# The end of a 128-tile Strassen matmul: where the last weight sets are put, how the last block of C21 is added, and how it is stored

## The chip, the cores and the metric

One NeuronCore of a Trainium2 chip runs the whole program. TensorE (PE) multiplies, VectorE (DVE) and ScalarE (ACT) scale, add and copy, SyncE (SP) issues the DMAs. The metric is the device time of one execution in microseconds (us). The kernel before takes 1450.54 us, the median of 3 runs from 1450.36 to 1450.79.

## The reference

`x` is 8 x 2048 x 2048 and `w` is 2048 x 2048, both float32. The cumulative sum of `x` along the sequence, less the same sum moved on by one place, is `x` again, so what is computed is a matrix product:

```python
cs = np.cumsum(x, axis=1)
diff = cs - np.concatenate([np.zeros((cs.shape[0], 1, cs.shape[2]), dtype=np.float32), cs[:, :-1, :]], axis=1)
return np.matmul(diff, w).astype(np.float32)
```

The kernel takes `x` as 16384 rows, that is 128 tiles of 128 rows, and multiplies them by `w`.

## The kernel before, in words

Four row tiles are done plainly in bf16. Then come 31 groups of four tiles (`g`, `g+1`, `h = g+2`, `h+1`), in float16 with a scale for each row. A group is one Strassen-Winograd step over 2 x 2 blocks: `A11`, `A12` are the two halves (in K) of tiles `g` and `h`, `A21`, `A22` those of `g+1` and `h+1`, and `B11` to `B22` the quarters of `w`. Products named P1 to P5 go one level further: `Quarters` makes each from seven quarter products (`slot(0)` to `slot(6)`), each of four 128 x 512 matmuls, and two products (T2 and T3) are plain, in pieces of four matmuls. So PE does 51 pieces of four matmuls in each group.

Weights of the inner level are differences of blocks of `w`. Most lie ready. One set at a time (`Q1`, `Q3` or `Q4`) is made on DVE just before it is needed (`give`, one 128 x 2048 subtraction) and written to `flow`, a buffer of four pieces that all these sets share. A set can be written when the matmuls that read the set before it are done.

Inside `Quarters`, `h[0]` is a bank that collects the quarter products 0, 2, 4 and 6. After product 0 ACT copies it to `g[0]` (`first`). After products 2 and 4 ACT copies what it holds so far to a lent buffer (`out2`, `out4`), and DVE adds those copies to `g[1]` and `h[1]` (`middle`, `last`). Product 6 changes `h[0]` for the last time, so it must come after `out4`.

The results of a group leave PSUM by scaled copies on ACT (`keep`, line 624), followed by scaled adds on DVE (`add`, line 635), and are stored by SP (`put`). The last group stores 128 x 512 pieces of 256 KB (line 655), the others 512 KB. In every group C21 of tile `h+1` is the last: ACT keeps `Y` in SBUF, and after product 6 of P4 DVE adds `P4.h` times the row scale. In the kernel before its half 0 is the last instruction of DVE, and its store the last of the program.

The order of the work is not that of the code. Every step is recorded with a label and an engine, and `emit` sorts all of them by a table of numbers (`places`), one list for each group: 0, 1, 2, 29, 30, 31 and one for all between. Group 30 is the last, and list 31 holds what is left of its end. In that order each engine runs its own steps strictly in turn; the framework adds the waits. Where DVE and ACT both touch one PSUM bank, it lets the later of the two wait for the earlier, for reads too.

These are the last steps of each engine in the kernel before, in their order (a bare name is of group 30):

```
PE   ... P4.2, S3h T3.1.0, P4.1, S3h T3.1.1, S3h T3.0.0, S3h T3.0.1, P4.4, P4.3, P4.5, P4.6
DVE  ... in4.Q3, P4.s3, P4.middle, P4.s4, C22h+Y.1, C22h+Y.0, P4.last, C21h+P4.h.1, C21g+P4.g.1, C21g+P4.g.0, C21h+P4.h.0
ACT  ... P4.out2, keep C21h.1, keep C21h.0, P4.out4, keep C21g.1
SP   ... put3.1.1 (C22h), put3.1.0, put-1.0.1 (C21h), put1.0.1 (C21g), put1.0.0, put-1.0.0 (C21h)
```

`S3h T3.1.x` fill bank `Y[1]` and `S3h T3.0.x` bank `Y[0]`; `P4.0`, `P4.2`, `P4.4`, `P4.6` fill `P4.h[0]`.

For the start of the last group these names matter too. `load7.0` brings half of the last row tile, `weigh7.0` sums it on ACT, `narrow7.0` makes it float16 and `turn7.0` transposes it by DMA. They belong to the tiles of group 30 but run at the end of group 29, between steps of both groups.

Of the kernel before, what the change touches and what calls it, by code (L numbers as in the profile page):

```python
# [10 lines left out]
def kernel(  # L11
# [103 lines left out]

    def record(label, engine, ask):
        at = seen[period[0], label] = seen.get((period[0], label), 0) + 1
        if at > 1:
            label = f"{label}#{at}"
        ops.append((period[0], label, engine, ask))  # L120

# [51 lines left out]
    def narrow_one(t, i):  # L173
        to, data, s = narrowed(t)[:, ds(i * NH, NH)], where[t][i], scales[t]
        record(
            f"narrow{role(t)}.{i}",
            "act",
            lambda: nc.scalar.activation(to, data, COPY, scale=s),  # L178
        )
        if i == 1 and t != PLAIN + 1:  # L180
            stage.append(where[t][1])
# [75 lines left out]
    def cast_x(q, a):  # L257
        to = resting(q, 0).bitcast(bf16).rearrange("p (a c) -> p a c", a=2)[:, a]
        src = resting(KH - 1 - q, a)
        record(f"cast x.{q}.{a}", "dve", lambda: nc.vector.tensor_copy(to, src))  # L260
        return to
# [13 lines left out]
    def turned(q, a, v, engine):  # L275
        to = xP[:, ds(2 * a, 2), ds(q * KQ, KQ), :].rearrange("p r k m -> p r (k m)")
        v = v.rearrange("p (r c) -> p r c", r=2)
        on = nc.scalar.copy if engine == "act" else nc.vector.tensor_copy
        record(f"turned x.{q}.{a}", engine, lambda: on(to, v))  # L279
# [30 lines left out]
    def taken(h, ko):  # L310
        src = rest(h, ko)
        to = wb[h, ko] = next(rings)
        record(f"cast w.{h}.{ko}", "act", lambda: nc.scalar.copy(to, src))
        largest(h, ko)
# [22 lines left out]
    def result(name, p, rows, columns, u=None):  # L337
        c = next(results_at)
        if u is None and name in ("out.0.1.0", "out.0.2.0"):
            record(f"{name}", "dve", lambda: nc.vector.tensor_copy(c, p))  # L340
        elif u is None:
            record(f"{name}", "act", lambda: nc.scalar.copy(c, p))  # L342
        else:
            record(f"{name}", "act", lambda: nc.scalar.activation(c, p, COPY, scale=u))
# [52 lines left out]
    for ko in range(KO - KQ):  # L397
# [20 lines left out]
        if ko == PART[-1]:  # L418
            for k in PART:
                part(k)  # L420
            record("part", "act", lambda: nc.scalar.copy(partial, banks[7]))
# [35 lines left out]
    def block(name, dst, a, h, k, engine):  # L457
        to, src = dst[k], whole[k][:, a, h, :].rearrange("p (n c) -> p n c", c=NB)
        if engine == "dve":
            ask = lambda: nc.vector.tensor_scalar(to, src, uinv, None, MUL)  # L460
        else:
            ask = lambda: nc.scalar.activation(to, src, COPY, scale=uinv)  # L462
        record(f"{name}.{k}", engine, ask)
# [159 lines left out]
    def keep_one(label, c, p, u):  # L623
        record(label, "act", lambda: nc.scalar.activation(c, p, COPY, scale=u))  # L624

    def copy(label, to, p):
        record(label, "act", lambda: nc.scalar.copy(to, p))  # L627
# [35 lines left out]
    class Seven:  # L663
# [16 lines left out]
        def give(self, name):  # L680

            p, q, op = {"Q1": ("t22", "Q2", SUB), "Q4": ("t21", "Q2", SUB), "Q3": ("Q2", "t11", SUB)}[name]
            if name == "Q4":
                less(f"{self.name}.{name}", passed, self.b[p], self.b[q])
            else:
                tensor(f"{self.name}.{name}", flow, self.wide[p], self.wide[q], op)
            self.b[name] = passed

        def spill(self, name):
# [3 lines left out]
            what = flow if self.b[name] is passed else self.wide[name]  # L693
# [122 lines left out]

    def group_plain(g):
# [69 lines left out]
        make_2(in_2)  # L887
# [16 lines left out]
        make_3(in_3)  # L904
# [18 lines left out]
    def all_seven(g):  # L923
        return g > PLAIN + 4

# [3 lines left out]
    def first_two(g):  # L929
        if g < END:  # L930
# [3 lines left out]
            if all_seven(g):  # L934
# [3 lines left out]
            ready[2] = Quarters("P2", ready["zz"], A12g, A12h, in_2, room(at + 1), False)  # L938

    def group(g):  # L940
        h = g + 2
        more = all_seven(g)
# [30 lines left out]
        if more:  # L973
# [29 lines left out]
        P5 = Quarters("P5", P2.banks, S1g, S1h, in_5, room(at))  # L1003
# [12 lines left out]
        if not more:  # L1016
            make_5(in_5)
        in_5.give("Q3")
# [15 lines left out]
        if not more:  # L1034
            make_1(in_1)
# [7 lines left out]
        P3 = Quarters("P3", P5.banks, S4g, S4h, in_3, room(at + 1))  # L1043
# [12 lines left out]
        in_3.give("Q1")  # L1056
# [20 lines left out]
        P4 = Quarters("P4", P3.banks, A22g, A22h, in_4, room(at))  # L1077
        P4.one()
        P4.two()
        in_3.give("Q3")  # L1080
        if not more:
            make_3(in_4)
# [19 lines left out]
        in_4.give("Q1")  # L1102
# [19 lines left out]
        in_4.give("Q3")  # L1122
# [25 lines left out]
        if next_g < END:  # L1148
            if all_seven(g + 4):
# [8 lines left out]
        C21h = keep("keep C21h", Y, vh, halves=[0])  # L1158
        add("C22h+Y", C22h, Y, vh, [0])
        keep("keep C21h", Y, vh, C21h, [1])  # L1160
        add("C22h+Y", C22h, Y, vh, [1])
        P4.slot(6)
        turn(next_l, [1])
# [3 lines left out]
        def tail():  # L1167
            add("C21h+P4.h", C21h, P4.h, vh, [0])
# [8 lines left out]
    for g in range(PLAIN + 4, END, 4):  # L1177
# [405 lines left out]
```

## Time and profile before

| what | value |
|---|---|
| median of 3 runs | 1450.54 us |
| span of the profiled execution, first to last instruction | 1449.2 us |
| PE busy | 1438.6 us, 99% |
| DVE busy | 1334.3 us, 92% |
| ACT busy | 1204.5 us, 83% |
| DMA, mean | 243 GB/s |
| last PE piece | from 1443.10 us |
| last store issued | at 1445.68 us |

The page gives the span of the execution that was profiled; of that execution no other time is given. The runs timed without a profile lie 1.3 us above the span. The page cuts the span into 40 slices, gives the share of each engine in each, and follows the chain of work that ended last. A timeline gives start and duration of each instruction, and in square brackets how long its engine had been idle before it and who ended that. One row may stand for several instructions of one line (`x4`): then its duration is that of the whole row, in which pipelined instructions overlap.

### The profile page before, as it was taken

To read this page: it belongs to the slowest core of one execution; us is meant where nothing else is said; L and a number is where in the kernel's file an instruction comes from. 1 tells how busy PE (TensorE), PEld (TensorE's weight loads), DVE (VectorE), ACT (ScalarE), POOL (GpSimd) and SP (SyncE) were. 2 spreads that over 40 slices of the span, in tenths; PEclk is the share of its full clock that TensorE was granted. 3 is DMA by queue.
4 is the path that set the end of the run, shared out by engine and by line. 5 is a ranking of instruction groups with operands and counts; after the bars stand their busy time and mean duration, and the time that the engine had idled before them with its cause. 6 is when DMAs were issued, how large, how long until landed. Compare 5 with 4: busy or idle time off the path is not lost.

```text
span 1449.2 us, 20358 instructions
## 1 busy us (share of the span) xinstructions
PE 1438.6 (99%) x6692; PEld 652.2 (45%) x6698; DVE 1334.3 (92%) x2345; ACT 1204.5 (83%) x1994; POOL 0.5 (0%) x5
## 2 busy tenths in 40 slices
PE   8999999999999999999999999999999999999998
PEld 4444444444444444444444444444444444444443
DVE  6999999999999999999999999999999999999988
ACT  5997888898888888888988888988888888889783
POOL 0000000000000000000000000000000000000000
PEclk9999999999999999999999999999999999999999
DMA  9999979899888999989998888998989998989973
GB/s 360 369 252 272 252 212 228 240 247 262 226 234 226 243 262 231 244 222 228 247 265 233 228 229 237 252 257 226 222 239 244 260 248 225 218 236 248 264 200 116
DMA packets 343930, 351.59 MB, mean 243 GB/s; under 512 B 270992, under 2 KB 270992, under 8 KB 343824
## 3 DMA queue, kind: packets, MB, share of 16 engines
q1 hardware_dynamic: 343824, 350.29, 89.4%
q8 instruction: 52, 0.85, 0.2%
q14 instruction: 54, 0.44, 0.1%
HBM read 150.99 MB, written 134.22 MB: 197 GB/s over the span
## 4 chain that ended last, share of the span: by engine, by line
PE 91%; issue 4%; DMA 2%; ACT 2%; DVE 1%; DVEq 0%; POOLq 0%; ACTq 0%; SPq 0%
PE b L610 61%; PE b L588 30%; DMA x<-F 1%; DMA F<-in_x_dram 1%; DVE W L460 1%; ACT waste L140 0%; DMA out_dram<-arena 0%; ACT W L462 0%; DVE arena L635 0%; ACT arena L624 0%; ACT F L178 0%; ACT arena L342 0%; ACT arena L178 0%; DVE arena L576 0%; DVE W L576 0%
## 5 line engine op out<-in xcount | busy, mean ns | idle before, releaser
L588 PE MATMUL b<-W,x 128*128 128x512 f16 x2144 | 518.1, 379 | 0.1
L635 DVE SCALAR_TENSOR_TENSOR arena<-b,tiny,arena 128x512 f32<-128x512 f32 x612 | 446.9, 745 | 16.0 <-PE b L610 4.8
L610 PEld LDWEIGHTS <-arena 128*128 128x128 f16 x2744 | 268.2, 98 | 325.4 <-DVE arena L576 6.3
L610 PE MATMUL b<-W,arena 128*128 128x512 f16 x1672 | 413.7, 379 | 0.8 <-DVE arena L576 0.4
L624 ACT ACTIVATE arena<-b,tiny 128x512 f32<-128x512 f32 x496 | 317.0, 684 | 35.4 <-PE b L588 14.9
L588 PEld LDWEIGHTS <-x 128*128 128x128 f16 x2144 | 209.7, 98 | 253.3 <-issue 0.3
L140 ACT ACTIVATE waste<-F,tiny 128x1024 uint8<-128x1024 f32 x246 | 283.9, 1154 | 15.6 <-DMA F<-in_x_dram 14.1
L178 ACT ACTIVATE F<-F,tiny 128x1024 f16<-128x1024 f32 x246 | 282.1, 1147 | 10.9 <-DVE tiny L163 9.4
L610 PE MATMUL b<-W,x 128*128 128x512 f16 x1192 | 287.5, 379 | 0.0
L610 PE MATMUL b<-arena 128*128 128x512 f16 x1072 | 261.6, 379 | 0.0
L610 PEld LDWEIGHTS <-x 128*128 128x128 f16 x1428 | 139.7, 98 | 168.5
L576 DVE TENSOR_TENSOR b<-b,arena 128x512 f32<-128x512 f32 x298 | 205.9, 691 | 5.7 <-ACT arena L627 2.0
L627 ACT COPY b<-b 128x512 f32<-128x512 f32 x149 | 85.5, 574 | 134.4 <-PE b L610 112.4
L627 ACT COPY arena<-b 128x512 f32<-128x512 f32 x298 | 170.2, 580 | 19.9 <-PE b L610 13.0
L576 DVE TENSOR_TENSOR arena<-W 128x2048 f16<-128x2048 f16 (+1 forms) x158 | 185.6, 1176 | 0.4 <-PE b L610 0.4
L576 DVE TENSOR_TENSOR arena<-x,x 128x512 f16<-128x512 f16 (+1 forms) x181 | 91.5, 506 | 50.1 <-PE b L610 50.1
L576 DVE TENSOR_TENSOR x<-x,x 128x1024 f16<-128x1024 f16 x124 | 85.2, 687 | 2.0
L576 DVE TENSOR_TENSOR arena<-W,arena 128x512 f16<-128x512 f16 (+1 forms) x157 | 85.9, 563 | 0.6 <-PE b L610 0.5
L576 DVE TENSOR_TENSOR arena<-arena 128x512 f16<-128x512 f16 x120 | 50.8, 424 | 13.7 <-PE b L610 11.8
L610 PE MATMUL b<-arena,x 128*128 128x512 f16 x236 | 60.3, 379 | 0.0
L324 PE MATMUL b<-arena 128*128 128x512 bf16 x234 | 53.5, 379 | 1.5 <-DVE arena L279 0.8
L576 DVE TENSOR_TENSOR arena<-x,arena 128x512 f16<-128x512 f16 x119 | 49.6, 417 | 0.6 <-PE b L610 0.6
(49 smaller groups left out, 503.6 us busy)
## 6 DMA issues: line engine op xcount, KB each, us to landing
F<-in_x_dram SPq DMA_DIRECT2D x246, 512.0 KB, 5.4
out_dram<-arena SPq DMA_DIRECT2D x240, 512.0 KB, 4.8
W<-in_w_dram SPq DMA_DIRECT2D x31, 512.0 KB, 9.5
out_dram<-arena SPq DMA_DIRECT2D x31, 256.0 KB, 2.7
W<-in_x_dram SPq DMA_DIRECT2D x16, 256.0 KB, 6.6
x<-F SPq DMA_TRANSPOSE x246, 4.4
arena<-in_x_dram SPq DMA_DIRECT2D x2, 512.0 KB, 5.1
W<-in_w_dram SPq DMA_DIRECT2D x2, 256.0 KB, 9.0
```

Source lines behind the costliest of these rows:

```text
L140: lambda: nc.scalar.activation(waste, data, ABS, bias=least, scale=1.0 / ROW, accum_out=m),
L178: lambda: nc.scalar.activation(to, data, COPY, scale=s),
L324: said = nc.tensor.matmul(to[n], xP[:, r, ko, :], b[:, ds(n * NB, NB)], start=(ko == 0), stop=(ko == KO - 1),)
L460: ask = lambda: nc.vector.tensor_scalar(to, src, uinv, None, MUL)
L576: record(label, "dve", lambda: nc.vector.tensor_tensor(dst, p, q, op))
L588: said = nc.tensor.matmul(to[n], a[k], b[k][:, n, :], start=(start and k == 0), stop=(k == KH - 1), skip_group_check=True,)
L610: said = nc.tensor.matmul(to, a[k], b[k], start=(start and k == 0), stop=(k == 3), skip_group_check=True)
L624: record(label, "act", lambda: nc.scalar.activation(c, p, COPY, scale=u))
L627: record(label, "act", lambda: nc.scalar.copy(to, p))
L635: label, "dve", lambda: nc.vector.scalar_tensor_tensor(c, p, u, c, MUL, ADD)
```

## The change

- In the last group the sets `in3.Q1`, `in3.Q3`, `in4.Q1` and `in4.Q3` are no longer written to `flow`, but each to a block of weights of its own that P1 and P2 have used and that no later group needs (`home`). In all other groups nothing changes here.
- Half 0 of `C21h` in the last group: ACT copies `Y[0]` unscaled to SBUF (`copy C21h`), DVE adds this to `P4.h[0]` in its bank (`C21h+P4.h0`) after `out4` and before product 6. After product 6 ACT scales and copies the left 256 columns of the bank (`end.0`), DVE the right 256 (`end.1`). Two stores of 128 x 256, 128 KB each, follow, one issued by ACT (`put end.0`), one by SP (`put end.1`). The scaled add of half 0 (`C21h+P4.h.0`) and its store of 256 KB are gone.
- The lists 29, 30 and 31 are new: in the last two groups the steps stand in another order on PE, DVE, ACT and SP. On PE the pieces are the same. Up to the first pieces of group 29 all four orders are as before.
- Helpers are rewritten so that a step can be recorded for either engine (`on_two`, `moved`), and products can be made plain (`plainly`, `made`); the tables in this kernel leave all engines and products as they were.

```diff
+        final = g + 4 >= END
+        over = [in_1.wide["t11"], in_1.wide["t21"], in_2.wide["t11"], in_2.wide["t21"]]
+        def home():
+            return over.pop(0) if final else flow
...
-        in_3.give("Q3")
+        if not P3.plain:
+            in_3.give("Q3", home())
...
+        if final:
+            C21h = free.pop(0)
+            copy("copy C21h", C21h[:, 0, :], Y[0])
+            add("C22h+Y", C22h, Y, vh, [0])
+            keep("keep C21h", Y, vh, C21h, [1])
+            add("C22h+Y", C22h, Y, vh, [1])
+            tensor("C21h+P4.h0", P4.h[0], P4.h[0], C21h[:, 0, :], ADD)
...
         def tail():
+            if final:
+                P4.last()
+                add("C21h+P4.h", C21h, P4.h, vh, [1])
+                put_half(C21h[:, 1, :], h + 1, 0, 1)
+                for i, engine in enumerate(("act", "dve")):
+                    columns = ds(i * NB // 2, NB // 2)
+                    c, p = C21h[:, 0, columns], P4.h[0][:, columns]
+                    record(f"end.{i}", engine, on_two(c, p, vh))
...
```

The last steps of each engine in the changed kernel, in their order:

```
PE   ... P4.0, S3g T3.0.0, P4.2, P4.1, S3g T3.0.1, P4.4, S3h T3.1.0, S3h T3.1.1, S3h T3.0.0, S3h T3.0.1, P4.5, P4.3, P4.6
DVE  ... P4.s3, P4.middle, C22g+X.0, P4.s4, P4.last, C22h+Y.1, C21h+P4.h.1, C22h+Y.0, C21h+P4.h0, C21g+P4.g.1, C21g+P4.g.0, end.1
ACT  ... P4.out2, P4.out4, keep C21g.0, keep C21h.1, copy C21h, keep C21g.1, end.0, put end.0
SP   ... put3.1.1, put-1.0.1, put3.1.0, put1.0.1, put1.0.0, put end.1
```

The waits that the framework adds: `copy C21h` waits for `C22h+Y.0` (same bank), `keep C21h.1` for `C22h+Y.1`, `P4.6` for `C21h+P4.h0`, and `end.1` for `end.0`.

Around the seam of groups 29 and 30 these orders are new (before, then after):

```
SP   before: load5.1, turn6.0, turn4.1, put0.1, turn6.1, put2.1, load7.0, load7.1, put1.1, turn5.1, put1.0, turn5.0
SP   after:  load5.1, turn4.1, put0.1, turn6.0, turn6.1, put2.1, load7.0, load7.1, turn5.0, turn5.1, put1.1
ACT  before: keep C21h.0, P4.out4, unit6, keep C21h.1, 30:P1.first, weigh7.0, weigh7.1
ACT  after:  P4.out4, weigh7.0, keep C21h.1, keep C21h.0, 30:P1.first, weigh7.1, 30:P1.out2
DVE  after:  C22h+Y.0, C21g+P4.g.0, P1.s2, 30:in1.Q4.0, C22h+Y.1, P2.s2, C21g+P4.g.1, 30:P4.last, ... 30:C11g+P2.g.0
PE   after:  29:P4.4, S3h T3.1.1, P4.3, P4.6, P4.5, then 30:P1.1, P1.0, P2.0, P1.2, P2.1, P1.3, ... P2.4, S2g T2.0.0, P5.0
```

`P5.0` of group 30 writes the bank that `C11g+P2.g.0` reads.

More of the change, by code (lines that the diff above doesn't have):

```diff
@@ L114 @@
     seen = {}
+    moved = {
+    }
     def record(label, engine, ask):
@@ L119, in record, with on_two @@
             label = f"{label}#{at}"
+        if isinstance(ask, dict):
+            if label in moved.get(period[0], ()):
+                engine = {"act": "dve", "dve": "act"}[engine]
+            ask = ask[engine]
         ops.append((period[0], label, engine, ask))
+    def on_two(to, src, scale=None):
+        if scale is None:
+            return {
+                "act": lambda: nc.scalar.copy(to, src),
+                "dve": lambda: nc.vector.tensor_copy(to, src),
+            }
+        return {
+            "act": lambda: nc.scalar.activation(to, src, COPY, scale=scale),
+            "dve": lambda: nc.vector.tensor_scalar(to, src, scale, None, MUL),
+        }
     def role(t):
@@ L335, with result @@
     results_at = iter(results * 2)
-    def result(name, p, rows, columns, u=None):
+    def result(name, p, rows, columns):
         c = next(results_at)
[L339 to L344, printed above, removed]
+        record(name, "dve" if name in ("out.0.1.0", "out.0.2.0") else "act", on_two(c, p))
         done.append(
@@ L420 @@
                 part(k)
[L421 removed]
+            record("part", "act", on_two(partial, banks[7]))
     for ko in range(KO - KQ, KO):
@@ L678, in room, with give @@
             return [spare.pop(0) for _ in range(4)]
-        def give(self, name):
+        def give(self, name, to=flow):
             p, q, op = {"Q1": ("t22", "Q2", SUB), "Q4": ("t21", "Q2", SUB), "Q3": ("Q2", "t11", SUB)}[name]
+            pieces = [to[:, k, :] for k in range(4)]
             if name == "Q4":
-                less(f"{self.name}.{name}", passed, self.b[p], self.b[q])
+                less(f"{self.name}.{name}", pieces, self.b[p], self.b[q])
             else:
-                tensor(f"{self.name}.{name}", flow, self.wide[p], self.wide[q], op)
-            self.b[name] = passed
+                tensor(f"{self.name}.{name}", to, self.wide[p], self.wide[q], op)
+            self.b[name] = pieces
         def spill(self, name):
@@ L692, in spill @@
             spilled.append(to)
-            what = flow if self.b[name] is passed else self.wide[name]
+            what = flow
             record(f"{self.name}.{name}.spill", "sp", lambda: nc.sync.dma_start(to, what))
@@ L815, in slot, with plainly, made @@
                 matmuls(*halves_of(f"{self.name}{name}", to, a, self.right, True)[at % 4])
+    def plainly(name, g):
+        return name in {PLAIN + 4: ('P1',)}.get(g, ())
+    making = {}
+    def made(name, inner, how):
+        if name not in making:
+            making[name] = True
+            how(inner)
     def group_plain(g):
@@ L972, in group @@
         P1.slot(1)
-        if more:
+        if not P1.plain:
             in_1.give("Q4")
@@ L1015, in group @@
         P1.slot(6)
-        if not more:
-            make_5(in_5)
-        in_5.give("Q3")
+        if not P5.plain:
+            made("P5", in_5, make_5)
+            in_5.give("Q3")
         C11h = keep("keep C11h", Y, uh, free.pop(1))
@@ L1033, in group @@
         total("S4g", S4g, A12g, S2g, SUB)
-        if not more:
-            make_1(in_1)
+        if not plainly("P1", g + 4):
+            made("P1", in_1, make_1)
+        if not plainly("P2", g + 4):
+            made("P2", in_2, make_2)
         go(2)
@@ L1101, in group @@
         P3.last()
-        in_4.give("Q1")
+        if not P4.plain:
+            in_4.give("Q1", home())
         scale_of(next_k)
@@ L1121, in group @@
             ready[1].two()
-        in_4.give("Q3")
+        if not P4.plain:
+            in_4.give("Q3", home())
         weigh(next_l, [0])
@@ L1157, in group @@
         turn(next_l, [0])
[L1158 to L1161, printed above, removed]
-        P4.slot(6)
+        if final:
[5 more added lines that the diff above has]
+            tensor("C21h+P4.h0", P4.h[0], P4.h[0], C21h[:, 0, :], ADD)
+        else:
+            C21h = keep("keep C21h", Y, vh, halves=[0])
+            add("C22h+Y", C22h, Y, vh, [0])
+            keep("keep C21h", Y, vh, C21h, [1])
+            add("C22h+Y", C22h, Y, vh, [1])
+        P4.slot(6)
+        if P4.plain and not plainly("P4", g + 4):
+            made("P4", in_4, make_3)
+        if P5.plain and not plainly("P5", g + 4):
+            made("P5", in_5, make_5)
+        if P3.plain and not plainly("P3", g + 4):
+            made("P3", in_3, make_3)
         turn(next_l, [1])
@@ L1167, in tail @@
         def tail():
+            if final:
[6 more added lines that the diff above has]
+                    record(f"end.{i}", engine, on_two(c, p, vh))
+                for i in range(2):
+                    columns = ds(i * NB // 2, NB // 2)
+                    c = C21h[:, 0, columns]
+                    record(
+                        f"put end.{i}",
+                        ("act", "sp")[i],
+                        lambda queue=(nc.scalar, nc.sync)[i], c=c, columns=columns: queue.dma_start(
+                            out2[ds((h + 1) * P, P), columns], c
+                        ),
+                    )
+                return
             add("C21h+P4.h", C21h, P4.h, vh, [0])
```

65 lines of the change are left out of this document (33 added, 32 removed), and 151 rows, old and new, of the table places.

## The prediction

> **What bounds the kernel now.** I read the page first: the shares of the engines, the slices and the chain that ended last.
>
> ```profile
> span 1449.2 us, 20358 instructions
> ...
> PE 1438.6 (99%) x6692; PEld 652.2 (45%) x6698; DVE 1334.3 (92%) x2345; ACT 1204.5 (83%) x1994; POOL 0.5 (0%) x5
> ...
> PE   8999999999999999999999999999999999999998
> ...
> PE 91%; issue 4%; DMA 2%; ACT 2%; DVE 1%; DVEq 0%; POOLq 0%; ACTq 0%; SPq 0%
> ```
>
> TensorE is full in every slice but the first and the last, and 91% of the chain is TensorE. The change leaves its matmuls as they are, so it can gain only at waits of TensorE and behind its last matmul, and it can lose anywhere in the last two groups. So I looked next at TensorE's timeline there.
>
> ```profile
> 1425.69 1.03 PE L588 MATMUL b<-W,x 128*128 128x512 f16 x4
> 1426.70 1.02 PE L610 MATMUL b<-W,arena 128*128 128x512 f16 x4
> ...
> 1426.08 0.57 ACT L627 COPY b<-b 128x512 f32<-128x512 f32 x1
> ...
> 1442.24 1.03 PE L610 MATMUL b<-W,arena 128*128 128x512 f16 x4
> 1443.10 1.03 PE L610 MATMUL b<-W,x 128*128 128x512 f16 x4
> ```
>
> A piece of four matmuls starts 0.86 us after the one before it (1442.24 to 1443.10) and is through after 1.03. The only wait is at 1426.70, 0.15 us late, behind a copy on ACT (P3.first) that ends at 1426.65. The last piece, P4.6, ends at 1444.13; 5.1 us of the span lie behind it. There DVE is the bound:
>
> ```profile
> 1439.60 0.69 DVE L576 TENSOR_TENSOR b<-b,arena 128x512 f32<-128x512 f32 x1
> 1440.20 0.41 DVE L576 TENSOR_TENSOR arena<-x,arena 128x512 f16<-128x512 f16 x1
> 1440.53 0.74 DVE L635 SCALAR_TENSOR_TENSOR arena<-b,tiny,arena 128x512 f32<-128x512 f32 x1
> 1441.43 0.75 DVE L635 SCALAR_TENSOR_TENSOR arena<-b,tiny,arena 128x512 f32<-128x512 f32 x1 [0.16 <-ACT arena L624]
> 1442.19 0.70 DVE L576 TENSOR_TENSOR b<-b,arena 128x512 f32<-128x512 f32 x1
> 1442.93 2.73 DVE L635 SCALAR_TENSOR_TENSOR arena<-b,tiny,arena 128x512 f32<-128x512 f32 x4
> ```
>
> The last row is the four last adds, back to back to 1445.66, of which the last needs P4.6. From these rows I take DVE's steps, start to next start: a scaled add 0.66 ((2.73 - 0.75) / 3), an f32 addition in PSUM 0.60 (1439.60 to 1440.20), a 512-wide f16 one 0.33 (1440.20 to 1440.53). Then come the store and the end:
>
> ```profile
> 1443.71 0.33 SPq L655 DMA_DIRECT2D out_dram<-arena  x1
> ...
> 1445.68 0.33 SPq L655 DMA_DIRECT2D out_dram<-arena  x1
> ...
> out_dram<-arena SPq DMA_DIRECT2D x1, 256.0 KB, 2.6
> SPq L1578 <- DMA out_dram<-arena: 2.1, 1, 2.1
> 1444.00:1445.00 1.00, 0.13 (x1) 0.00 (x0) 1.00 (x3) 0.00 (x0) 0.00 (x0) 1.00 0.46 174
> 1445.00:1446.00 1.00, 0.00 (x0) 0.00 (x0) 0.65 (x1) 0.00 (x0) 0.00 (x0) 1.00 1.04 383
> 1446.00:1447.00 1.00, 0.00 (x0) 0.00 (x0) 0.00 (x0) 0.00 (x0) 0.00 (x0) 1.00 1.05 352
> 1447.00:1448.00 1.00, 0.00 (x0) 0.00 (x0) 0.00 (x0) 0.00 (x0) 0.00 (x0) 0.86 0.39 139
> ```
>
> Issued at 1445.68, landed 2.6 later, at 1448.3; SP waits for it, and 0.9 us of closing steps follow. In the windows (last two numbers: share of the DMA engines, GB/s) they work 0.46 of the us from 1444, all of the next two and 0.39 of the last: 2.85 us from 1444.54 to 1447.39, for the four stores issued from 1443.71 on. Data starts 0.83 after issue, a store takes 0.71, and the landing is 0.9 after the data. So two things are level here: DVE gives a store each 0.66 us, and the DMA engines need 0.71.
>
> **The change part by part.** The sum stands against the span of 1449.2; the median of the runs, 1450.54, is 1.3 above it, and I add that.
>
> Helpers, and steps recorded for two engines: no instruction changes, 0 us.
>
> Sets in dead blocks: the same four subtractions, 0 of work.
>
> ```profile
> L576 DVE TENSOR_TENSOR arena<-W 128x2048 f16<-128x2048 f16 x10 | 12.2, 1219 | 0.2 <-PE b L610 0.2
> ```
>
> In the last two groups DVE idled 0.2 us ahead of ten of them, on readers of `flow`, and TensorE hid it; so I credit nothing between 0 and 0.2. Uncovered, a set made late costs 1.22. What the blocks free is order. The 0.15 at 1426.70 I take as gone, since P3.0 and so its copy come earlier against P3.2: P4.6 would then start at 1442.95.
>
> Half 0 of C21, up to P4.6. These groups and rows carry it:
>
> ```profile
> L624 ACT ACTIVATE arena<-b,tiny 128x512 f32<-128x512 f32 x33 | 21.5, 688 | 7.2 <-PE b L588 3.9 <-PE b L610 3.2
> L627 ACT COPY arena<-b 128x512 f32<-128x512 f32 x20 | 11.5, 580 | 8.8 <-PE b L610 8.0 <-DVE b L576 0.8
> L576 DVE TENSOR_TENSOR b<-b,arena 128x512 f32<-128x512 f32 x21 | 14.6, 694 | 2.4 <-ACT arena L627 1.5 <-ACT arena L624 0.6
> 1440.71 0.69 ACT L624 ACTIVATE arena<-b,tiny 128x512 f32<-128x512 f32 x1 [1.04 <-PE b L588]
> ```
>
> The keep on ACT at 1440.71 ends at 1441.40, and the add of the same bank starts on DVE at 1441.43: two readers of one bank go one after the other. In the new order S3h T3.1.1 is the sixth piece from the end (starts 1442.95 - 5 x 0.863 = 1438.64) and ends at 1439.67. Behind it stand, each 0.03 after its releaser: C22h+Y.1 on DVE (0.75) to 1440.45, keep C21h.1 on ACT (0.69) to 1441.17, C21h+P4.h.1 on DVE from 1441.20; C22h+Y.0, whose bank is ready at 1441.40, comes behind it in DVE's queue, at 1441.86, and ends at 1442.61; copy C21h on ACT (0.58) to 1443.22; the new addition (0.69) to 1443.94. P4.6 starts at about 1443.97 and not at 1442.95: TensorE waits 1.0 us, with nothing queued behind P4.6 on TensorE. It ends at 1445.00.
>
> The halves: `end.0` and `end.1` are on one bank, and `end.1` has a wait for `end.0`. No row has 256 columns. Rows on both sides:
>
> ```profile
> 1398.45 0.30 ACT L167 ACTIVATE tiny<-tiny 128x1 f32<-128x1 f32 x1
> 1404.17 0.16 DVE L163 RECIPROCAL tiny<-tiny 128x1 f32<-128x1 f32 x1 [0.18 <-ACT tiny L161]
> ```
>
> ACT: between 0.30 and 0.69, I take 0.46; DVE: between 0.16 and 0.75, I take 0.42 (both near the middle, as the column count is). So `end.0` runs 1445.03 to 1445.49, `end.1` 1445.52 to 1445.94 (by the bounds together 1445.5 to 1446.5). The last issue is at 1445.97, before 1445.68: 0.3 later. Behind `end.0` only its store is queued on ACT, behind `end.1` nothing on DVE.
>
> The Trainium skill, page "PSUM — Partial Sum Buffer", section "PSUM bank collisions raise a hardware error", speaks against copying one bank by two engines: they must not be on it at once in the same 32 partitions, readers and other columns included. By that rule the halves stand in a row and the end is at 1445.94; side by side they would end at 1445.49. The trace agrees with the rule: the add at 1441.43 waited for the keep.
>
> The stores: C21g's two adds start on DVE behind the new addition, at 1443.86 and 1444.52 (keep C21g.1 on ACT, behind copy C21h, ends at 1443.8), and are issued at about 1444.63 and 1445.30. With the two halves 768 KB flow from 1445.46 (0.83 after issue), three times 0.71, to 1447.6; the landing is at 1448.5, 0.2 later than before. The last store then lands 2.5 after its issue. No row has 128 KB or a store of ACT's queue; bounds for it are 1.9 (2.6 less a queue and half a transfer, 0.35 each) and 4.8:
>
> ```profile
> out_dram<-arena SPq DMA_DIRECT2D x240, 512.0 KB, 4.8
> ```
>
> The end is from -0.4 to +2.5, and I take +0.2, near the row of 256 KB.
>
> [...]
>
> The new order at the seam of the two groups. On SP `turn6.0` now stands behind `put0.1`, which waits for a DVE add, and `load7.0` behind both transposes. Before:
>
> ```profile
> 1384.78 3.64 SPq L195 DMA_TRANSPOSE x<-F  x2
> 1389.03 0.35 SPq L643 DMA_DIRECT2D out_dram<-arena  x1
> 1389.47 1.50 SPq L195 DMA_TRANSPOSE x<-F  x1
> 1391.79 0.35 SPq L643 DMA_DIRECT2D out_dram<-arena  x1
> 1392.23 4.09 SPq L132 DMA_DIRECT2D F<-in_x_dram  x2
> F<-in_x_dram SPq DMA_DIRECT2D x1, 512.0 KB, 5.2
> F<-in_x_dram SPq DMA_DIRECT2D x1, 512.0 KB, 4.0
> F<-in_x_dram SPq DMA_DIRECT2D x1, 512.0 KB, 7.2
> 1401.29 1.15 ACT L140 ACTIVATE waste<-F,tiny 128x1024 uint8<-128x1024 f32 x1
> ```
>
> Two transposes take SP 3.64. With `put0.1` at about 1389.5 (P3.5 is one piece later in the new order), `load7.0` goes out at 1394.0 instead of 1392.23 and lands 4.0 to 7.2 later; its own row (the first of the three) had 5.2, which gives 1399.2. On ACT `weigh7.0` (1.15) now stands ahead of keep C21h.1 (0.69), and C22h+Y.1 on DVE waits for that keep: 1401.1. DVE is free for it from 1400.53 (in1.Q4.0, behind the first matmul of P1.1). From its start to the end of C11g+P2.g.0 are 21 instructions: 4 scaled adds at 0.66 and the last at 0.75, 7 long additions at 0.60, 8 short at 0.33, a reciprocal: 10.3 us. P5.0, 37 pieces before the last, should start at 1411.0 and needs that add. Started at 1400.53 the chain ends at 1410.9, in time by 0.1; from 1401.1 it ends at 1411.4, and TensorE waits 0.45. So each us by which `load7.0` lands after 1398.8 is a us of TensorE: 0 at 4.0, 0.45 at 5.2, 2.4 at 7.2. I take 0.45, the row of the same load. The other moved steps (transposes of group 29's tiles, weighs, keeps) I walked in the same way, and no margin came out below zero; several are under 0.1, so some tenths more can show.
>
> Sum: seam +0.45, end +0.2 (the 0.15 and the 1.0 are in it): span 1449.85, time 1451.2, 0.05% above before. About 0.2% (2.9 us) is what a measurement can tell, so my forecast is no change.
>
> **The rivals.**
> - No seam wait: `load7.0` lands within 4.8 us. For it: the load of 4.0; against it: the two transposes ahead in the queue. Span 1449.4, time 1450.7; with the last store at its lower bound 1450.1.
> - Slower: the late `load7.0` holds ACT, ACT holds DVE, DVE holds TensorE. It decides from a landing 7.5 us after issue (1401.5: 2.7 of wait on top of the 0.2); the longest of the three rows has 7.2, which gives 1453.1. At 8.3 us the time is 1454.2. Against it: the row of this very load has 5.2.
> - Faster by over 0.2%: from 1444.0, the earliest end of TensorE, a half copy 0.46, a store 2.5 and 0.9 of closing give 1447.9, 1449.2 as a time; 1448.6 with the store's lower bound. Even with every wait gone it stays inside the 0.2%.
> - The bank addition costs more than 1.0 of TensorE, if copy C21h finds ACT busy: 1451.9 with one more keep (0.69) in front. For it: keep C21g.1 stands next to it in ACT's order; against it: behind, not ahead.
>
> **How the numbers follow.** Forecast with small waits of 0.1 to 2 us at the seam or P4.6: 0.60 (the fourth rival, 0.1, lies in it), 1450.8 to 1452.8. No seam wait: 0.31. Slower by over 0.2%: 0.07. Faster by over 0.2%: 0.02, for things not seen here. The range 1449.9 to 1452.9 leaves out the 0.07 and the upper end of the bounds. Within 0.2%: 0.60 + 0.31 = 0.91.
>
> **What would show it.** P4.6 starting 1.0 us behind P4.3's slot, its releaser the DVE addition. `end.1` starting after `end.0` ends. P5.0 of the last group starting late, with C11g+P2.g.0 as releaser and a DVE wait before C22h+Y.1. Landing of `load7.0` and of the two small stores. I would be wrong if ACT's store lands 3 us or more after its issue, if the waits at the seam come from another step, or if DVE is late elsewhere in the last group.

## The result and the profile after

The changed kernel takes 1453.32 us, the median of 11 runs from 1452.85 to 1454.82; the kernel before, run beside it, 1450.25 us (11 runs, 1449.28 to 1450.79). The ratio is 1.0023, with a 95% interval of 1.0014 to 1.0031. It is slower by 3.1 us, and outside the range that was given (to 1452.9).

The page of the changed kernel, three of the places that were shown of before:

```profile
span 1452.0 us, 20371 instructions
...
PE 1441.0 (99%) x6698; PEld 652.2 (45%) x6698; DVE 1334.2 (92%) x2346; ACT 1204.4 (83%) x1995; POOL 0.5 (0%) x5
...
PE 90%; issue 5%; DVE 3%; DMA 2%; ACT 1%; SPq 0%; POOLq 0%; DVEq 0%; ACTq 0%
```

The span is 2.8 us longer. The page can't say where: TensorE is at 99% in both, and a per cent of the chain is 14.5 us. TensorE's timeline of the changed kernel can. A piece of four is on time when it starts 0.86 us after the one before it:

```profile
1368.32 1.03 PE L592 MATMUL b<-W,x 128*128 128x512 f16 x4
1370.07 1.02 PE L614 MATMUL b<-W,arena 128*128 128x512 f16 x4 [0.73 <-DVE arena L639]
1370.93 1.03 PE L592 MATMUL b<-W,x 128*128 128x512 f16 x4
1371.99 1.24 PE L614 MATMUL b<-W,arena 128*128 128x512 f16 x5
...
1401.63 1.67 PE L614 MATMUL b<-W,x 128*128 128x512 f16 x7
1403.83 1.89 PE L614 MATMUL b<-arena 128*128 128x512 f16 x8 [0.52 <-ACT b L132]
...
1411.64 1.03 PE L592 MATMUL b<-W,x 128*128 128x512 f16 x4
1413.21 1.89 PE L614 MATMUL b<-W,arena 128*128 128x512 f16 x8 [0.54 <-DVE arena L639]
...
1444.40 1.03 PE L614 MATMUL b<-W,x 128*128 128x512 f16 x4
1446.33 1.02 PE L614 MATMUL b<-W,x 128*128 128x512 f16 x4 [0.90 <-DVE b L580]
```

The bracket gives the idle time after the modelled end of the piece before; what a wait costs is the start less the start that was due. P5.1 of group 29 was due at 1369.18 and starts at 1370.07: 0.89 late. P5.2, due at 1371.79, is another 0.20 late, and a piece at 1374.64 another 0.07: together **1.16 in group 29**. Seven matmuls take 1.51 us, so P1.2 of the last group was due at 1403.14 and is 0.68 late (by the unrounded starts); P5.0 is 0.70 late, and two pieces between and after them lose 0.05 and 0.09: together **1.52 at the seam**. P4.6 is **1.06** late. The kernel before had one wait of 0.15 in the same stretch.

What follows P4.6 has become shorter: from its start to the end of the span before 1449.2 - 1443.10 = 6.1, after 1452.0 - 1446.33 = 5.7, that is 0.4 less. The balance: 1.16 + 1.52 + 1.06 - 0.15 - 0.4 = 3.2; the span grew by 2.8. The 0.4 that is left lies ahead of group 29, where the order is the same in both; by so much, and by twice as much, profiled executions differ there (the run with the dead blocks alone), so the waits within a trace are compared here rather than whole spans.

Who was late is seen on DVE, in the timeline of the changed kernel:

```profile
1365.37 0.69 DVE L580 TENSOR_TENSOR b<-b,arena 128x512 f32<-128x512 f32 x1
1367.13 0.69 DVE L580 TENSOR_TENSOR arena<-x,x 128x1024 f16<-128x1024 f16 x1 [1.07 <-DMA x<-F]
...
1369.27 0.74 DVE L639 SCALAR_TENSOR_TENSOR arena<-b,tiny,arena 128x512 f32<-128x512 f32 x1
...
1402.63 0.75 DVE L639 SCALAR_TENSOR_TENSOR arena<-b,tiny,arena 128x512 f32<-128x512 f32 x1 [1.24 <-ACT arena L136]
...
1412.41 0.74 DVE L639 SCALAR_TENSOR_TENSOR arena<-b,tiny,arena 128x512 f32<-128x512 f32 x1
...
1445.58 0.70 DVE L580 TENSOR_TENSOR b<-b,arena 128x512 f32<-128x512 f32 x1 [0.65 <-ACT arena L132]
...
1447.90 0.48 DVE L137 TENSOR_SCALAR arena<-b,tiny 128x256 f32<-128x256 f32 x1 [0.31 <-ACT arena L136]
```

The row at 1367.13 is `S1h` of group 29, the sum of the two halves of tile h+1. It waits 1.07 us for a transpose, and C11g+P2.g.1 (1369.27), which P5.1 needs, stands behind it. At 1402.63 C22h+Y.1 waits 1.24 for a keep on ACT; C11g+P2.g.0 (1412.41), which P5.0 needs, stands behind that. At 1445.58 is the new bank addition, at 1447.90 `end.1`. ACT, in the timeline of the same kernel:

```profile
1400.78 1.15 ACT L158 ACTIVATE waste<-F,tiny 128x1024 uint8<-128x1024 f32 x1 [2.90 <-DMA F<-in_x_dram]
...
1401.93 1.24 ACT L136 ACTIVATE arena<-b,tiny 128x512 f32<-128x512 f32 x2
1403.21 0.57 ACT L132 COPY b<-b 128x512 f32<-128x512 f32 x1
...
1444.96 0.58 ACT L132 COPY arena<-b 128x512 f32<-128x512 f32 x1 [1.47 <-DVE arena L639]
...
1447.39 0.47 ACT L136 ACTIVATE arena<-b,tiny 128x256 f32<-128x256 f32 x1 [1.26 <-PE b L614]
1447.89 0.37 ACTq L1231 DMA_DIRECT2D out_dram<-arena  x1
```

`weigh7.0` (1400.78) waits 2.9 us for the load; behind it go two keeps and then P1.first (1403.21), for which P1.2 waited. `end.0` is at 1447.39, and `end.1` follows at 1447.90, 0.04 after it ends. Last, SP in the timeline of the same kernel:

```profile
1361.12 3.76 SPq L209 DMA_TRANSPOSE x<-F  x2
...
1394.56 1.29 SPq L150 DMA_DIRECT2D F<-in_x_dram  x2
1395.90 7.03 SPq L209 DMA_TRANSPOSE x<-F  x2
...
1448.41 0.33 SPq L1231 DMA_DIRECT2D out_dram<-arena  x1
```

and the landings among its DMA issues (the last number is us from issue to landing):

```profile
F<-in_x_dram SPq DMA_DIRECT2D x1, 512.0 KB, 6.2
...
out_dram<-arena ACTq DMA_DIRECT2D x1, 128.0 KB, 3.0
out_dram<-arena SPq DMA_DIRECT2D x1, 128.0 KB, 2.6
```

The second transpose of the first row is `turn7.1`, the one that `S1h` waits for; it is issued at 1362.64, 4.5 before `S1h` starts. `load7.0` goes out at 1394.56 and lands 6.2 later. The last store is issued at 1448.41 and lands 2.6 later.

### The profile page after: what moved, and what is told of

Its sections match the earlier page's. It is cut to its first block, busy times and chain, and to the rows that moved or that the text cites. A ratio compares the mean times of both kernels' runs of the same rounds, so it can differ in the third digit from the quotient of the medians.

```text
span 1452.0 us, 20371 instructions
## 1 busy us (share of the span) xinstructions
PE 1441.0 (99%) x6698; PEld 652.2 (45%) x6698; DVE 1334.2 (92%) x2346; ACT 1204.4 (83%) x1995; POOL 0.5 (0%) x5
## 4 chain that ended last, share of the span: by engine, by line
PE 90%; issue 5%; DVE 3%; DMA 2%; ACT 1%; SPq 0%; POOLq 0%; DVEq 0%; ACTq 0%
PE b L614 60%; PE b L592 30%; DMA F<-in_x_dram 1%; DVE W L137 1%; DMA x<-F 1%; DVE W L547 1%; DVE arena L639 0%; DVE arena L580 0%; ACT waste L158 0%; DVE b L580 0%; ACT arena L136 0%; ACT F L136 0%; DVE x L580 0%; DVE W L580 0%; SPq L209 0%
## 5 line engine op out<-in xcount | busy, mean ns | idle before, releaser
L614 PE MATMUL b<-arena 128*128 128x512 f16 x1056 | 257.4, 379 | 0.5 <-ACT b L132 0.5
L132 ACT COPY arena<-b 128x512 f32<-128x512 f32 (+1 forms) x318 | 184.0, 589 | 24.8 <-PE b L614 14.4
L580 DVE TENSOR_TENSOR arena<-W 128x2048 f16<-128x2048 f16 (+1 forms) x154 | 180.7, 1174 | 0.5 <-PE b L614 0.3
```

Of the source, the lines that this page charges most:

```text
L132: "act": lambda: nc.scalar.copy(to, src),
L580: record(label, "dve", lambda: nc.vector.tensor_tensor(dst, p, q, op))
L614: said = nc.tensor.matmul(to, a[k], b[k], start=(start and k == 0), stop=(k == 3), skip_group_check=True)
```

## The experiments

Seven kernels start from the changed one, the last two from the kernel before. The table gives each run's time (median), its ratio to the kernel before (95% interval), the waits of TensorE in group 29, at the seam and at P4.6, and the tail (P4.6's start to the end of the span). All in us. An interval is some 1.3 us wide to each side, so where two kernels differ by less than a microsecond, the waits in the traces carry the reading and the times only fit it.

| kernel | time | ratio | group 29 | seam | P4.6 | tail |
|---|---|---|---|---|---|---|
| changed | 1453.32 | 1.0023 [1.0014, 1.0031] | 1.16 | 1.52 | 1.06 | 5.67 |
| copy first | 1452.66 | 1.0018 [1.0009, 1.0028] | 0.89 | 1.59 | 0 | 5.84 |
| S1h without its wait | 1452.27 | 1.0016 [1.0007, 1.0026] | 0 | 1.42 | 1.07 | 5.62 |
| weigh behind | 1452.75 | 1.0018 [1.0008, 1.0027] | 1.35 | 0.90 | 1.07 | 5.63 |
| transpose ahead | 1451.98 | 1.0014 [1.0005, 1.0024] | 0.44 | 0.26 | 1.07 | 5.68 |
| three mended | 1450.22 | 0.9999 [0.9990, 1.0008] | 0.05 | 0.18 | 0 | 5.84 |
| one end | 1453.48 | 1.0023 [1.0014, 1.0032] | 1.29 | 1.23 | 1.07 | 5.41 |
| three mended, one end | 1450.18 | 0.9999 [0.9990, 1.0008] | 0.05 | 0.20 | 0 | 5.94 |
| before + new C21 end | 1450.67 | 1.0002 [0.9993, 1.0011] | 0 | 0 | 0 | 6.57 |
| before + dead blocks | 1449.97 | 0.9999 [0.9990, 1.0008] | 0 | 0 | 0 | 6.09 |

The last two keep the 0.15 of the kernel before at P3.2 (at 1425.97 and 1425.93), which stands in none of the columns.

**Copy C21h and the bank addition ahead of C22h+Y.0.** The changed kernel with two places moved. ACT's own order stays as it is (`copy C21h` still follows `keep C21h.1`); what changes is that the copy comes before `C22h+Y.0` on their common bank, and so no longer waits for that add, and that the bank addition stands ahead of it on DVE:

```diff
-  'copy C21h': 173, ... 'C21h+P4.h0': 175,
+  'copy C21h': 171.5, ... 'C21h+P4.h0': 171.8,
```

> The changed kernel with two steps of its last list moved: copy C21h and the addition C21h+P4.h0 stand ahead of C22h+Y.0. The first theory says that the changed kernel's 1.06 us of TensorE ahead of the last piece come from the queue: the copy waits for an add of DVE that itself stands behind another. Then the copy starts as soon as its bank is filled, P4.6 waits under 0.2 us, all other waits of TensorE stay, and the span falls by about 1.0 us. The rival says that the three links after the bank is filled (copy, addition, last piece) are too long for the two pieces in between in any order: then P4.6 still waits 0.5 us or more and the span falls by under 0.5.

P4.6's wait is gone; the end of DVE in the timeline of this run:

```profile
1443.50 0.70 DVE L580 TENSOR_TENSOR b<-b,arena 128x512 f32<-128x512 f32 x1
1444.11 2.06 DVE L639 SCALAR_TENSOR_TENSOR arena<-b,tiny,arena 128x512 f32<-128x512 f32 x3
1446.08 0.47 DVE L137 TENSOR_SCALAR arena<-b,tiny 128x256 f32<-128x256 f32 x1
```

The addition starts at 1443.50 and P4.6 at 1444.41. The wait of 1.06 was that chain: the copy had stood behind an add of DVE that stood behind another. The tail has grown by 0.17: P4.6 is earlier, but `end.1` now stands behind three scaled adds. Of the 0.9 that wait and tail make together the median shows 0.7.

**S1h of group 29 from halves that landed long before.** This leaves the right sum for `S1h` out in that one group: it adds `A11h` and `A12h`, which have no late transpose, instead of `A21h` and `A22h`.

```diff
-  total("S1h", S1h, A21h, A22h, ADD)
+  total("S1h", S1h, *((A11h, A12h) if period[0] == 29 else (A21h, A22h)), ADD)
```

> The changed kernel, but in group 29 the sum S1h is made from two halves of x that landed long before (A11h and A12h, so the results of that group are not the reference's). The theory says that the 1.16 us of waits of TensorE in group 29 (0.89, 0.20 and 0.07) come from S1h: it now stands earlier in DVE's queue and waits there for the transpose turn7.1 of the group before. Then these waits fall to under 0.2 in sum and the span falls by about 1.0 us. One rival says that DVE is behind by its own work in that stretch: then the waits stay above 0.8. Another says that what is won here is lost at the seam, where the load's landing does not move with TensorE: the waits in group 29 go, those of the last group's start grow, and the span falls by under 0.4.

All three waits of group 29 are gone, and the time falls by 1.05 us against 1.16 in the trace. The seam gave nothing of it back (1.42 after 1.52), so the rival that the loss would reappear there fell, and so did the one that DVE is behind by its own work. DVE has no gap ahead of `S1h` now (first row) in the timeline of this run:

```profile
1365.11 0.68 DVE L580 TENSOR_TENSOR arena<-x,x 128x1024 f16<-128x1024 f16 x1
...
1367.25 0.74 DVE L639 SCALAR_TENSOR_TENSOR arena<-b,tiny,arena 128x512 f32<-128x512 f32 x1
```

**weigh7.0 behind P1.first on ACT.**

```diff
-  'weigh7.0': 1618,
+  'weigh7.0': 1633.5,
```

> The changed kernel with one step moved on ACT: weigh7.0 stands behind P1.first of the last group, as before the change, so keep C21h.1 no longer stands behind it. The theory says that the 1.5 us of waits at the start of the last group (0.68 at P1.2, 0.70 at P5.0 and two small ones) come from the landing of load7.0, handed on by ACT's queue to keep C21h.1 and P1.first and from there to DVE. Then P1.2 does not wait, P5.0 waits under 0.3, and the span falls by 1.0 to 1.4 us. The rival says that the 21 instructions of DVE up to C11g+P2.g.0 are too long whatever ACT does: P5.0 still waits 0.5 or more and the span falls by 0.7 at most.

P1.2 starts on time, but the waits move on, in the timeline of this run (TensorE, and DVE in the last row):

```profile
1404.26 1.03 PE L614 MATMUL b<-W,x 128*128 128x512 f16 x4
1405.43 1.02 PE L614 MATMUL b<-W,arena 128*128 128x512 f16 x4
...
1410.62 1.03 PE L592 MATMUL b<-W,x 128*128 128x512 f16 x4
1412.01 1.24 PE L614 MATMUL b<-W,arena 128*128 128x512 f16 x5 [0.36 <-DVE arena L639]
...
1404.44 0.69 DVE L580 TENSOR_TENSOR arena<-x,x 128x1024 f16<-128x1024 f16 x1 [0.42 <-DMA x<-F]
```

P1.4 is 0.31 late, as P1.out2 now stands behind both weighs on ACT, and P5.0 is still 0.52 late: DVE now stops at `S1g` (last row) for `turn5.1`, another transpose of the same queue. The wait at P5.0 is as long as the rival said, but not for the rival's reason, DVE's 21 instructions. So 0.6 of the seam's 1.5 went with ACT's order, and for the rest a next reason stood ready. What ACT's order alone is worth stays open: in this execution `load7.0` landed 7.5 us after its issue, and not 6.2 as in the changed kernel.

**turn6.0 ahead of put0.1 on SP, as in the kernel before**, so that the load isn't held behind two transposes.

```diff
-  'put0.1': 1577, ... 'turn6.0': 1579,
+  'turn6.0': 1576.5, 'put0.1': 1577,
```

> The changed kernel with one step moved on SP: turn6.0 stands ahead of put0.1, as before the change, so that load7.0 is issued about 1.5 us earlier. The theory says that the landing of load7.0 moves with its issue (5 to 6 us after it), so the 1.5 us of waits at the start of the last group fall to 0.5 or less and the span falls by about 1.0 us. The rival says that the DMA engines are full there, so that the load lands when it did: waits and span as in the changed kernel, within 0.3.

SP and ACT in the timeline of this run:

```profile
1393.10 1.21 SPq L150 DMA_DIRECT2D F<-in_x_dram  x2
...
1398.70 1.15 ACT L158 ACTIVATE waste<-F,tiny 128x1024 uint8<-128x1024 f32 x1 [1.63 <-DMA F<-in_x_dram]
```

The load goes out 1.5 earlier than in the changed kernel (1393.10, 1394.56) and `weigh7.0` runs 2.1 earlier, so the rival, that it lands when it did, falls; 1.52 of wait shrink to 0.26. Not all of the 2.1 is the edit's: TensorE itself was 0.8 earlier here, 0.1 ahead of group 29 and 0.72 in it. Against TensorE the load goes out 0.6 earlier and lands 1.25 earlier, as it took 5.6 us instead of 6.2; the seam's wait fell by 1.26. So nearly all of that wait hung on when this load lands, which one transpose moved. In group 29, where nothing was edited, this execution lost 0.44 instead of 1.16 (DVE in the same timeline):

```profile
1366.30 0.69 DVE L580 TENSOR_TENSOR arena<-x,x 128x1024 f16<-128x1024 f16 x1 [0.35 <-DMA x<-F]
```

`S1h` starts 3.8 us after `turn7.1` is issued here, against 4.5 in the changed kernel (the transpose landed after 3.7 us and after 4.4): that wait hangs on the landing of a transpose, and its size differs between executions (P5.1 was late by 0.89, 0.82, 1.08, 1.02 and 0.18 in five kernels with the same order there).

**All three mended**: copy first, transpose ahead, and in group 29 another order on DVE. `S1h` stands behind P1.last, `P5.s1` behind C11g+P2.g.1, and `S3h` and `S2h` right behind in5.Q3 (`S3h` further back than in the changed kernel, `S2h` further ahead). Beside the two edits above:

```diff
-  'S1h': 1457, ... 'P1.last': 1458, ... 'S3h': 1459, ... 'P5.s1': 1460, ... 'S2h': 1509,
+  'S1h': 1458.5, ... 'P1.last': 1456.6, ... 'S3h': 1468.3, ... 'P5.s1': 1461.5, ... 'S2h': 1468.6,
```

> The changed kernel with all three orders mended: copy C21h and the bank addition ahead of C22h+Y.0; turn6.0 ahead of put0.1 on SP; and in group 29 S1h and P5.s1 around C11g+P2.g.1, S3h and S2h behind in5.Q3, so that S1h comes when its transpose has landed. The theory says that the waits of TensorE in the last two groups are all of the loss: their sum falls from 3.7 us to under 0.6, and the span comes to within 0.5 us of that of the kernel before, 1448.7 to 1449.7. The rival says that the gains do not add up, since each one lets another transfer be met earlier: waits of 1.2 us or more stay and the span is above 1450.2.

1450.22 us beside 1450.48 of the kernel before: no difference, and 0.23 of waits are left. `S1h` still waits 0.50 for its transpose, but no instruction stands between it and the add that P5.1 needs (three did), and TensorE feels 0.05. Within the interval (1.3 us to each side) the three waits are the whole loss. The span of the profiled execution, 1447.6, lies below the 1448.7 to 1449.7 that was expected, by more than the waits can give; single spans differ by so much. Beyond the three waits no worth of the change is seen in the times, though TensorE runs the last group's end without a wait, as its timeline in this run shows:

```profile
1440.90 1.89 PE L614 MATMUL b<-W,x 128*128 128x512 f16 x8
```

This row is P4.3 and P4.6 in one, eight matmuls without a gap.

**The end in one piece**: ACT copies all 512 columns, SP stores them at once.

```diff
-                for i, engine in enumerate(("act", "dve")):
...
-                    record(f"end.{i}", engine, on_two(c, p, vh))
...
+                c, p = C21h[:, 0, :], P4.h[0]
+                record("end.0", "act", on_two(c, p, vh))
+                record("put end.1", "sp", lambda: nc.sync.dma_start(out2[ds((h + 1) * P, P), ds(0, NB)], c))
```

> The changed kernel with the end of half 0 done by one engine and one store: ACT scales and copies all 512 columns, SP stores 256 KB. The theory says that two engines on one bank in a row (0.47 and 0.48 us) and two small stores win nothing against one copy of 0.69 and one store, since the DMA engines are full until some 1450.0 either way: last store issued 0.2 to 0.3 us earlier against the end of P4.6, span the same within 0.2 us. The rival says that the smaller stores land sooner: the span grows by 0.3 us or more.

ACT and SP in the timeline of this run:

```profile
1447.27 0.69 ACT L136 ACTIVATE arena<-b,tiny 128x512 f32<-128x512 f32 x1 [1.25 <-PE b L614]
...
1447.98 0.34 SPq L1223 DMA_DIRECT2D out_dram<-arena  x1
```

One copy of 0.69 us is done 0.69 after it starts; the two halves, 0.47 and 0.48 one after the other, 0.99 after. The tail is 5.41 against 5.67: the split loses 0.26 in the trace. In the times that is not to be seen (1453.48 beside 1453.32).

**Three mended and the end in one piece**, to see if there is a version that beats both kernels.

> The kernel with all three waits mended, and its end in one piece: ACT copies all 512 columns of the bank and SP stores them as 256 KB; the last step of DVE is gone. Theory (the two halves and the two small stores lose at the end, and when P4.6 comes early the right half stands behind two adds on DVE): ACT is free at P4.6's end, its copy of 0.69 us is done 1.76 us behind P4.6's start, against 2.15 for the right half in the mended kernel, but SP is still issuing the store before it; issue 1.8 to 2.1 behind P4.6's start instead of 2.21, landing 2.6 later. The tail from P4.6's start to the end of the span is 5.4 to 5.7 us instead of 5.84, the span 1447.2 to 1447.5 us, the time 1449.7 to 1450.1, ratio to the kernel before 0.9995 to 1.0000. Rival (the split pays once it does not follow the halves in a row, since a half store is through sooner): the tail is 6.0 or more and the span 1447.8 or more.

There is none here: 1450.18 beside 1450.17 of the kernel before. The tail is 5.94, outside what either theory said. ACT's copy is done at 1444.72, but the store goes out at 1445.18 (SP in the timeline of this run):

```profile
1442.00 3.08 SPq L659 DMA_DIRECT2D out_dram<-arena  x4
1445.18 0.40 SPq L1223 DMA_DIRECT2D out_dram<-arena  x1
```

With P4.6 early, SP is still issuing the four stores before it until 1445.08, and the last of them waits for DVE's last add of C21g (it ends at 1444.73). The end is DVE's queue of scaled adds again, whichever engine copies the last half.

**The new C21 end alone**, in the order of the kernel before:

```diff
-  C21h = keep("keep C21h", Y, vh, halves=[0])
+  copy("copy C21h", C21h[:, 0, :], Y[0])
...
+  tensor("C21h+P4.h0", P4.h[0], P4.h[0], C21h[:, 0, :], ADD)
```

and behind P4.6 the two halves and two small stores of the changed kernel.

> The kernel before, in its own order, with only the new end of C21: copy, bank addition, two scaled halves, two small stores. There the copy stands ahead of C22h+Y.0. The theory says that the bank addition costs TensorE nothing in that order (it is done by about 1442.9, P4.6 is due at 1443.1), and that the addition makes DVE's last steps about 0.3 us later: no wait at P4.6 above 0.1 us, span up by 0.1 to 0.4 us. The rival says that the bank addition as such costs about 1 us: P4.6 waits 0.5 us or more, and the span grows by 0.5 or more.

DVE, and TensorE's last piece, in the timeline of this run:

```profile
1441.46 1.30 DVE L576 TENSOR_TENSOR b<-b,arena 128x512 f32<-128x512 f32 x2
1442.80 2.07 DVE L635 SCALAR_TENSOR_TENSOR arena<-b,tiny,arena 128x512 f32<-128x512 f32 x3
1444.78 0.48 DVE L1184 TENSOR_SCALAR arena<-b,tiny 128x256 f32<-128x256 f32 x1
...
1442.37 1.03 PE L610 MATMUL b<-W,x 128*128 128x512 f16 x4
```

The addition (the first of the row of two) runs beside the piece ahead of P4.6, which starts on time at 1442.37. So the bank addition need not cost TensorE anything; it did in the new order, where `copy C21h` stood behind two adds of DVE. But one more instruction stands in DVE's queue: its last step ends 2.89 after P4.6's start instead of 2.56, and the tail is 6.57 instead of 6.09. In the times no difference is seen (1450.67 beside 1450.48).

**The dead blocks alone**, in the order of the kernel before:

```diff
-  in_3.give("Q1")
+  in_3.give("Q1", home())
```

and the same for the other three sets.

> The kernel before, in its own order, with only the four sets of the last group written to dead blocks of weights. The theory says that this changes nothing: waits of TensorE in the last two groups 0.3 us at most, span within 0.3 us. The rival says that the sets land on blocks whose readers or whose place in memory cost time: DVE's four subtractions longer than 1.22 us or waits of TensorE behind them, span up by 0.5 us or more.

1449.97 us, ratio 0.9999, the same single wait of 0.15: no difference. The span of its profile is 1448.4 against 1449.2 of the kernel before, with the same waits in group 29 and behind it and the same tail: by as much as 0.8 us profiled executions differ without a reason in these groups.

## Why the prediction was wrong

The span was forecast at 1449.85 and is 1452.0, 2.15 more. By the prediction's terms: group 29 +1.16, seam +1.07 (1.52 instead of 0.45), P4.6 +0.06 (1.06 instead of 1.0), tail +0.24 (5.67 instead of 1449.4 - 1443.97 = 5.43), and -0.36 from ahead of group 29; the sum is 2.17. The 1.3 us that the prediction added for the time set a median beside the span of another execution; where a run lists both, its time lies 1.7 to 2.0 above its own span. That did not make the error: the times differ from the forecast by 2.1 too.

- **The step that failed: "The other moved steps ... I walked in the same way, and no margin came out below zero".** One did, by 1.0 us. In the new order `S1h` of group 29 stands ahead of P1.last and C11g+P2.g.1 on DVE. In the kernel before it ran here, with no wait (DVE's and SP's timelines of before, and the landing among the DMA issues):

```profile
1370.43 0.68 DVE L576 TENSOR_TENSOR arena<-x,x 128x1024 f16<-128x1024 f16 x1
...
1363.03 2.27 SPq L195 DMA_TRANSPOSE x<-F  x1
...
x<-F SPq DMA_TRANSPOSE x1, 4.4
```

  There the transpose had been issued 7.4 us before, at 1363.03, and landed 4.4 us after its issue. In the changed kernel it landed after 4.4 us too, so the transfer is no slower; DVE is there sooner:

```profile
1362.64 2.24 SPq L209 DMA_TRANSPOSE x<-F  x1
...
x<-F SPq DMA_TRANSPOSE x1, 4.4
```

  DVE comes to `S1h` at 1366.06, 3.4 us after the issue. DVE stops, and everything behind it with it. The prediction shows no working for this walk, so what it took for this landing is not known; with the 4.4 of the kernel before, the margin comes out at 3.4 - 4.4, a microsecond below zero. The run with other halves in `S1h` showed the cause: 1.05 us. The Trainium skill, page "PSUM — Partial Sum Buffer", section "Engine vs sequencer instructions", says that the queues of ScalarE and VectorE are strictly first in, first out; the trace agrees: from the time at which DVE comes to `S1h` to the start of C11g+P2.g.1 it takes 3.21 us with the wait (1366.06 to 1369.27) and 2.14 without it (1365.11 to 1367.25), though nothing in that add had changed.
- **The term that was mis-sized: the seam, 0.45.** The mechanism was right: the load went out at 1394.56 (forecast 1394.0), held ACT at `weigh7.0`, ACT held C22h+Y.1, and that P5.0. But it landed 6.2 us after its issue, not 5.2. By the prediction's own rule (each us after 1398.8 is a us of TensorE) `weigh7.0`, at 1400.78, would give 1.98, less the 0.8 by which TensorE was itself behind (1.16 - 0.36), 1.2. Measured were 1.43 up to P5.0 and 0.09 at a later piece: the 21 instructions of DVE took 10.5 us (1402.63 to 1413.15), not 10.3. P1.2's wait of 0.68, behind a P1.first that stood behind the same weigh on ACT, was named by no step of the prediction; it lies inside the 1.43, since P5.0 was due later by as much. The row taken for the landing was that of the very load in the kernel before, but there it had not been issued behind two transposes in a row. It landed 4.9 to 5.2 us after its issue in the three kernels with the order of before, 5.4 to 5.6 in the three with `turn6.0` ahead, and 5.9 to 7.5 in the five with the changed order. In the changed kernel and the seven made from it `load7.1` also follows half a microsecond behind it, in the other three 3.8; how much of the difference that makes was not tried. The rival for slower is this mechanism with a landing of 7.5 us or more; alone it did not go so far, and with group 29 on top the time passed the 0.2% all the same.
- **The bank addition: right.** P4.6 waits 1.06 (forecast 1.0) with the DVE addition as releaser, by the chain that was named; with the copy and the addition ahead of C22h+Y.0 the wait is gone.
- **The halves: right.** 0.47 and 0.48 (forecast 0.46 and 0.42), in a row. The Trainium skill, page "PSUM — Partial Sum Buffer", section "PSUM bank collisions raise a hardware error", has them not be on one bank at once; as the framework orders them, `end.1` starts 0.04 after `end.0` ends, and the copy in one piece (0.69) is the shorter.
- **The end: nearly right.** The last issue is 2.08 after P4.6's start (forecast 2.0), and the landing 2.6 later (forecast 2.5). The store of ACT's queue, issued 0.5 earlier, landed 3.0 later, at about the same time (1450.9, 1451.1). A landing of 3 us was one of the signs of being wrong; it cost nothing.
- **Dead blocks and helpers at 0: right**, by the run with the blocks alone. The 0.15 at 1426.70 is gone, as forecast.
- **The range and the chances.** The range's upper end lies near the time for a landing of the load at 7.2. It had no room for DVE being late in group 29, and the signs of being wrong looked for that in the last group alone. That several small waits, each with a margin under 0.1, would open together was told ("some tenths more can show") but not counted. A chance of 0.07 for slower was too little for an order in which several margins were known to be near zero.

## What to carry to other kernels

When steps are moved ahead on an engine that runs strictly in turn, look for each moved step at what it reads, and at the landing of the DMA behind that: a step that came 7.4 us after a transpose's issue and now comes 3.4 after it stops everything behind it. A landing time belongs to a place in the queue, not to a transfer: the same load took 4.9 to 5.2 us in the old place and 5.9 to 7.5 in the new. And on a kernel whose busiest engine is at 99%, work out the margin of every moved step, and count those near zero together, not only the likeliest of them.

## What the runs showed of the hardware

- A half copy is not half a copy: 256 columns out of PSUM, with the row scale, took 0.47 us on ACT and 0.48 on DVE, 512 columns 0.69 on ACT. Halved between two engines, one after the other, the copy takes 0.3 us longer than whole.
- A store of 128 KB lands hardly sooner than one of 256 KB: as SP's last store it took 2.6 to 2.7 us from issue to landing in seven executions, and 256 KB in its place (the end in one piece) 2.7. The store of ACT's queue took 3.0 us in the changed kernel and 2.4 to 3.0 in the seven.
- The issue of one transpose, `turn5.1`, kept SP for 2.5 to 4.0 us in the eight executions in which it follows `turn5.0`, and `turn7.1` landed 3.7 to 4.6 us after its issue in eleven. What makes them differ was not tried.
